# Second layer's conditioning columns as tensor-engine products inside the recurrence

## The chip, the cores and the metric

One core of a Trainium2 chip runs the whole program. The metric is device time in microseconds (us) of one execution. Engine names in this text: PE is TensorE (matmul), PEld its weight loads, DVE is VectorE, ACT is ScalarE, POOL is GpSimd, SP is SyncE, whose queue carries nearly all loads.

## What is computed

A decoder trunk of two layers on 256 tokens of width 1024, all in float32. Each layer is a mixer and a mixture of experts (MoE), each with a gated residual. The conditioning vector c (1024 numbers) enters through one product per layer:

```python
cond = jax.nn.silu(c)
for layer in range(DEPTH):
    mod = cond @ ada_w[layer] + ada_b[layer]          # (1024) @ (1024, 6144)
    sh1, sc1, g1, sh2, sc2, g2 = jnp.split(mod, 6, axis=-1)
    h = modulate(rms_norm(x, norm_mix[layer]), sh1, sc1)
    y = ...                                           # the layer's mixer
    x = x + g1[:, None, :] * y
    h = modulate(rms_norm(x, norm_ffn[layer]), sh2, sc2)
    x = x + g2[:, None, :] * grouped_moe(h, ...)
return rms_norm(x, final_norm)
```

The second layer's mixer is a linear recurrence over the tokens (RWKV-7) beside a multi-scale pooling; both are concatenated and mapped by one output projection. `grouped_moe` has 16 experts, two per token.

## The kernel before

**Conditioning.** The 6144 outputs of one layer are 12 groups of 512 (`n` = 0 to 11), and a group is four columns of the tile `modc`, with the feature on the partition. `ada(l, n)` (L194) loads a group as two tiles of 128 x 2048 (1 MB each). For each of four halves DVE multiplies 128 x 1024 weights by `cond`, which lies broadcast over the partitions, and sums along the row (L200). GpSimd then adds the bias (L204). `ada_pieces` (L206) gives the same as four pieces that the mixer hands out one at a time, each pinned behind an instruction of the recurrence. In the second layer groups 0 to 2 are done in the first layer's mixer and group 3 before its MoE. Groups 4 to 11 are done in `mixer1`: 4 and 5 are the gate of the mixer (g1), 6 and 7 sh2, 8 and 9 sc2, 10 and 11 g2.

**Order.** PE and SP run in the order in which the program is written. DVE, ACT and POOL are put in order by the tile scheduler, except where `issue_after` pins an instruction. Tiles come from rotating buffers; a load waits on SP until the buffer's last reader is done.

**`mixer1` (L1199).** Projections of the tokens (products of three split parts, L437), then decay, keys and scores, then the recurrence in four chunks `c` of 64 tokens. `each` (L1427) is the small product of the recurrence: eight products of 64 x 64, 16 records in the trace, all at L1431. The order from L1609 on is: bonus and pool products, `tok_v` and `c_r`; then two rounds (m = 16, 32) of four `level_a` and four `level_b`, in which PE and DVE answer each other; then `c_u` and `c_w` for four chunks; then `c_h`, `c_s`, `c_y`, `c_g`, `c_q` and `head_norm` chunk by chunk.

**Fill.** `Fill` (L305) is a queue of units of PE work with an estimated cost each. `run(us)` emits units until their costs reach `us`. `pace(us, every)` adds up `us` and emits one unit when the sum is over `every`. The units here are bonus and pool products (0.5 each) and units of the output projection (`OutProj.units`, 0.86 each: one product of 512 columns, L363). The projection has 16 units for the first 128 tokens (`ou`) and 16 for the others (`ou1`); the last eight of each need the finished recurrence. `heat(n)` (L177) is n products of zeros on PE.

**Then** `into_moe` (L843) takes the last eight units of `ou1` as `us`, transposes x, routes the tokens and gathers them; `moe` (L950) runs eight pairs of experts. Its weights are loaded ahead into 19 buffers and one more as these come free.

```python
            for c in range(4):
                ins = level_a(c, m, st)
                fill.pace(0.65, 0.75)
                if c % 2 and todo:
                    todo.popleft()(ins)          # one quarter of an ada group
```

Of the kernel before, what the change touches and what calls it, by code (L numbers as in the profile page):

```python
# [11 lines left out]
F32 = mybir.dt.float32  # L12
# [3 lines left out]
AF = mybir.ActivationFunctionType  # L16
OP = mybir.AluOpType
# [79 lines left out]
def trunk(ctx: ExitStack, tc: tile.TileContext, A, out):  # L97
# [58 lines left out]
    def load_consts(pool, g, eng):  # L156
        cons[g] = pool.tile([128, _CW[g]], F32, name=g)
        eng.dma_start(cons[g], A[g])

    load_consts(con, "c_all", nc.scalar)  # L160

    def K(name):
        g, o, n = _COFF[name]
# [7 lines left out]
    V.memset(epsc[:, 1:2], LNX_EPS)  # L171
    junk = con.tile([128, 1], F32, name="junk")
    junk2 = con.tile([128, 512], BF, name="junk2")
    zb = con.tile([128, 128], BF, name="zb")
    V.memset(zb, 0.0)

    def heat(n):  # L177

        if n:
            t = ps(4, 128)  # L180
            for _ in range(n):
                mm(t, zb, zb[:, None, :].to_broadcast([128, 4, 128]), start=True, stop=True)
# [8 lines left out]
    def ada_load(l, n):  # L191
        return [stream(A["ada_w"][l, n, h]) for h in range(2)]

    def ada(l, n, tiles=None, h0=0, cs=(0, 1)):  # L194

        for h, w in enumerate(tiles or ada_load(l, n), h0):
            for c in cs:
                ws = w[:, c * D:(c + 1) * D]
                k = n * 4 + h * 2 + c
                V.scalar_tensor_tensor(ws, ws, 1.0, cond, op0=OP.mult, op1=OP.mult, accum_out=modc[:, l, k:k + 1])  # L200
        if h == 0 or c == 0:
            return
        o = V_ADAB + l * 48 + n * 4
        G.tensor_tensor(modc[:, l, n * 4:n * 4 + 4], modc[:, l, n * 4:n * 4 + 4], vec[:, o:o + 4], op=OP.add)  # L204

    def ada_pieces(l, n):  # L206

        tiles = ada_load(l, n)

        def piece(h, c, after):  # L210
            with tc.issue_after(after):
                ada(l, n, [tiles[h]], h, (c,))

        return [lambda after, h=h, c=c: piece(h, c, after) for h in range(2) for c in range(2)]

    def ada_col(l, j, ct=None):
        v = modc[:, l, j * 8:j * 8 + 8]
        return v if ct is None else v[:, ct:ct + 1]

    class Rms:  # L220

# [621 lines left out]
    def into_moe(l, us, tmp):  # L843

        norm = Norm(l, 1)
        for h in range(2):
            norm.ab(h)
        route = Route(norm)
        gb2 = act.tile([128, D], F32, name="gb", tag="gb")
        gu = gate_units(l, 5, gb2)  # L850
        us = deque(u for _, u in us)
        n = len(us)

        def run(n):
            for _ in range(n):
                us.popleft()()

        if l == 0:
            for h in range(2):
                norm.rms.square(0, h)  # L860
                route.transposes(0, h)
            run(max(0, n - 12))
            for h in range(2):
                route.logits(0, h)
            route.score(0)
            norm.split_lo(0)
            route.choose(0)
            run(len(us) - 4)
            route.place(0)
            for _, u in gu:  # L870
                u()
            route.transposes(1, 0)
            norm.rms.square(1, 0)
            run(2)

            Pp = picks(route, 0, (0,))
            run(2)
            route.logits(1, 0)
            preload(AF.Sqrt, norm.rms.ss[:, 1, 0:1])
            pgs = [ps(2, 256) for _ in range(4)]  # L880
            for ct in range(4):
                gather_mm(norm, pgs, Pp, ct, 0, ct % 2 == 0)
            route.transposes(1, 1)
            for ct in range(4, 8):
                gather_mm(norm, pgs, Pp, ct, 0, ct % 2 == 0)
            norm.rms.square(1, 1)
            route.logits(1, 1)
            route.score(1)
            route.choose(1)
            heat(14)  # L890
            route.place(1)
            ada(1, 3)
        else:
            def tr(tt, h):
                norm.rms.square(tt, h)
                route.transposes(tt, h)

            tr(0, 0)
            tr(0, 1)
            run(4)  # L900
            for h in range(2):
                route.logits(0, h)
            route.score(0)
            norm.split_lo(0)
            route.choose(0)
            run(4)
            tr(1, 0)
            route.logits(1, 0)

            preload(AF.Sqrt, norm.rms.ss[:, 1, 0:1])  # L910
            pgs = [ps(2, 256) for _ in range(4)]
            tr(1, 1)
            route.logits(1, 1)
            route.score(1)
            route.place(0)
            Pp = picks(route, 0, (0,))
            route.choose(1)
            for ct in range(8):
                gather_mm(norm, pgs, Pp, ct, 0, ct % 2 == 0)
            for _, u in gu:  # L920
                u()
            heat(4)
            route.place(1)
        return norm, route, gb2, Pp, pgs

# [24 lines left out]
    def moe(l, norm, route, gb, Pp0, pgs0):  # L950
# [62 lines left out]
        def s_gu(p):  # L1013
            XT = st[p][0]
            res = []
            for nm in ("moe_g", "moe_u"):
                ws = {(h, e): None for h in range(2) for e in range(2)}
                for h in range(2):
                    for e in range(2):
                        ws[h, e] = stream_w(nm, p, h, e)  # L1020
                pg = ps(512)
                for kt in range(8):
                    for e in range(2):
                        mm(pg[64 * e:64 * e + 64, :], XT[:, kt, 64 * e:64 * e + 64], ws[kt // 4, e][:, (kt % 4) * 512:(kt % 4 + 1) * 512],  # L1024
                           start=kt == 0, stop=kt == 7)
                res.append(pg)
            sg = mp.tile([128, 512], F32, name="sg", tag="sg")
            P.activation(sg, res[0], AF.Silu)  # L1028
            V.tensor_tensor(sg, sg, res[1], op=OP.mult)  # L1029
            sgs.append(sg)  # L1030

# [167 lines left out]
    def mixer1(rms, xs, gs_, after):  # L1199
# [67 lines left out]
        kk, sq = big("kk"), big("sq")  # L1267
        for ct in range(4):
            P.activation(sq[:, ct], kR[:, ct], AF.Square, scale=vc(V_KK, ct))
        rest = deque(range(4, 12))  # L1270
        ada(1, rest.popleft())
        gs_.append(Parts(1792, 512, ((None, None), (None, None)), (V, V)).split())

        sg, av, gg = big("sg"), big("av"), big("gg")
# [260 lines left out]
        def c_h(c):  # L1535
            Sst["p"] = t = ps(4, 64)
            each(t, 1, lambda p, h, own, other: KB[:, c, h, p], lambda p, h, own, other: VU[:, c, h, p], c == 0)
# [37 lines left out]
                    gs_[4].split((c + 1) // 2)  # L1575
        solved = []
        gb = buf["vR"]
        todo = deque()
        for _ in range(3):
            todo.extend(ada_pieces(1, rest.popleft()))  # L1580
        st = {}
        spent, steps = 0, 0

# [25 lines left out]
        step(fill.all())  # L1609
        op = OutProj(lambda kt: gg[:, kt] if kt < 4 else oB[:, kt - 4], "wout1", gb).load(1)  # L1610
        ou, ou1 = op.units(0), op.units(1)
        todo[0](solved[0])
        todo.popleft()
        fill.add([(0.5, lambda ct=ct: bonus(ct)) for ct in range(4)])
        fill.add([(0.5, lambda g=g: pool_unit(g)) for g in range(4)])
        fill.add(ou[:8] + ou1[:8])
        for u in [lambda cs=cs: tok_v(cs) for cs in ((0, 1), (2, 3))] + [lambda c=c: c_r(c) for c in range(4)]:
            step(fill.run(0.9) + 1)
            u()
            if len(todo) > 8:  # L1620
                todo.popleft()(solved[0])
        step(1e6)
        fill.run(5.7)
        for m in (16, 32):
            for c in range(4):
                ins = level_a(c, m, st)
                fill.pace(0.65, 0.75)
                if c % 2 and todo:
                    todo.popleft()(ins)
                elif m == 16 and c == 0:  # L1630
                    for k in range(4):
                        out_mask(k)
            for c in range(4):
                ins = level_b(c, m, st)
                fill.pace(0.65, 0.75)
                if c % 2 and todo:
                    todo.popleft()(ins)
        while todo:
            todo.popleft()(ins)
        for c in range(4):  # L1640
            c_u(c)
            if c:
                c_w(c)
            fill.run(0.5)
        ada(1, rest.popleft())
        op.load(0)
        c_h(0)
        c_s(0)
        c_y(0)
# [7 lines left out]
        c_h(1)  # L1657
        c_s(1)
        c_y(1)
        ada(1, rest.popleft())  # L1660
        c_q(3)
        fill.run(1)
        head_norm(1)
# [1 line left out]
        c_s(2)  # L1665
        fill.add(gate_units(1, 2, gb) + ou[8:])
        c_y(2)
        ada(1, rest.popleft())
        fill.run(2.5)
        head_norm(2)  # L1670
        c_y(3)
        fill.run(1)
        head_norm(3)
        ada(1, rest.popleft())
        fill.run(1)
        fill.all()
        after(ou1[8:], buf["uu"])
# [29 lines left out]
def pack(i):  # L1707
# [15 lines left out]
    A["router_b"] = f(i["router_b"])  # L1723
    A["final_norm"] = f(i["final_norm"])
    aw = i["ada_w"].reshape(2, D, 12, 2, 2, 128)
    A["ada_w"] = f(aw.transpose(0, 2, 3, 5, 4, 1).reshape(2, 12, 2, 128, TW))

    def groups(w, sizes):
# [37 lines left out]
```

## Time and profile before

| | |
|---|---|
| runs | 815.93, 809.97, 811.97 us; median 811.97 |
| profiled execution | 816.05 us, of which the span from first to last instruction is 814.3 us |
| PE busy | 745.0 us (91% of the span) |
| DVE busy | 430.5 us (53%) |
| ACT busy | 227.6 us (28%) |
| DMA | 291.34 MB, mean 358 GB/s |
| mean granted TensorE clock | 0.975 |

The stretches of the second layer in the span: projections and scores from about 411 us, the recurrence from about 507 to 569 us, `into_moe` to 597 us, the second MoE to 796 us, the final norm to the end. Times in rows are us from the span's start. A fp32 product is two records of PE. Rows that say "issue" are time in which the engine waited for nothing that the profile shows.

### The profile page before, as it was taken

The numbers are of one execution on the slowest core, as the hardware profiler recorded it, in microseconds if no ns is written. First come the engines' busy times: TensorE is split into PE (matmuls) and PEld (weight loads), VectorE is DVE, ScalarE is ACT, GpSimd is POOL, SyncE is SP. The second block draws the span as 40 slices with busy tenths as digits, with TensorE's granted clock in tenths as the row PEclk, the third lists the DMA queues.
The fourth block names the chain that finished last, engine by engine and source line by source line (L and its number), as shares of the span: only waits on it lengthen the run. The fifth ranks groups of instructions, "written<-read, shape, count | busy, mean of one in ns | idle before, by whom it ended". The sixth has DMA issues, their size and how long they took to land. (4 is left out here: it accounts for less than half of the span.)

```text
span 814.3 us, 12038 instructions
## 1 busy us (share of the span) xinstructions
PE 745.0 (91%) x4814; PEld 416.3 (51%) x4815; DVE 430.5 (53%) x969; ACT 227.6 (28%) x459; POOL 9.1 (1%) x32
## 2 busy tenths in 40 slices
PE   0998989998999999999979988998899999999993
PEld 0556766546344353443358988565543535335331
DVE  5657669965114342143468978798621531334325
ACT  3021323434111020120267644312621202112012
POOL 0000000000000000000000000000000000000000
PEclk9999989999999999999999989999899999999997
DMA  9999977999899999999667285587979999999981
GB/s 360 423 424 427 425 278 272 346 385 427 343 427 427 424 427 425 427 427 426 287 232 297 104 310 210 207 299 306 415 310 425 428 425 426 426 428 425 427 345 54
DMA packets 42688, 291.34 MB, mean 358 GB/s; under 512 B 4864, under 2 KB 5504, under 8 KB 8448
## 3 DMA queue, kind: packets, MB, share of 16 engines
q1 hardware_dynamic: 41760, 288.07, 86.4%
q10 hardware_dynamic: 864, 2.40, 0.8%
q8 instruction: 42, 0.69, 0.3%
q14 instruction: 22, 0.18, 0.1%
HBM read 289.40 MB, written 1.05 MB: 357 GB/s over the span
## 5 line engine op out<-in xcount | busy, mean ns | idle before, releaser
L1024 PE MATMUL ps<-w,XT 128*64 128x512 f32 x1024 | 223.1, 594 | 0.0
L1024 PEld LDWEIGHTS ps<-w,XT 128*64 128x64 f32 x1024 | 73.5, 137 | 145.7 <-issue 144.7
L200 DVE SCALAR_TENSOR_TENSOR w<-w,cond 128x1024 f32<-128x1024 f32 x96 | 114.5, 1218 | 10.8 <-ACT cond L148 6.3
L1029 DVE TENSOR_TENSOR sg<-sg,ps 128x512 f32<-128x512 f32 x16 | 11.0, 687 | 198.6 <-PE ps L1024 198.6
L1056 PE MATMUL ps<-w,HT 128*64 128x512 f32 x512 | 113.8, 596 | 1.3 <-ACT HT L1043 1.3
L1056 PEld LDWEIGHTS ps<-w,HT 128*64 128x64 f32 x512 | 35.2, 137 | 70.5 <-issue 62.9
L363 PE MATMUL ps<-w,slab 128*128 128x512 f32 x128 | 60.7, 613 | 0.0
L437 PE MATMUL ps<-hT,wr 128*128 128x256 f32 x288 | 54.9, 293 | 5.2 <-DVE wr L391 3.7
L1070 DVE SCALAR_TENSOR_TENSOR Y<-ps,gw,Y 128x512 fp32r<-128x512 f32 x32 | 24.0, 751 | 61.7 <-ACT Y L1069 61.7
L1069 ACT ACTIVATE Y<-ps,gw 128x512 fp32r<-128x512 f32 x32 | 22.0, 686 | 101.0 <-PE ps L1056 101.0
L437 PEld LDWEIGHTS ps<-hT,wr 128*128 128x128 f32 x288 | 46.3, 198 | 6.7 <-ACT wr L389 3.1
L374 DVE TENSOR_TENSOR x<-x,ps 128x512 f32<-128x512 f32 x72 | 46.3, 681 | 0.3
L568 PE MATMUL ps<-hT,w 128*128 128x256 f32 x192 | 46.3, 399 | 0.0
L373 DVE TENSOR_TENSOR ps<-ps,gb 128x512 f32<-128x512 f32 x64 | 41.5, 692 | 2.5 <-PE ps L1085 2.4
L437 PE MATMUL ps<-lo,wr 128*128 128x256 f32 x144 | 41.6, 289 | 0.1
L1085 PE MATMUL ps<-Y,CT 128*128 128x512 f32 x128 | 39.1, 422 | 2.8 <-ACT Y L1069 1.7
L568 PEld LDWEIGHTS ps<-hT,w 128*128 128x128 f32 x192 | 37.5, 200 | 6.2 <-issue 0.8
L482 PE MATMUL ps<-w,hT 128*128 128x512 f32 (+1 forms) x96 | 37.0, 546 | 0.3 <-ACT hT L271 0.2
L1028 ACT ACTIVATE sg<-ps 128x512 f32<-128x512 f32 x16 | 9.6, 597 | 92.3 <-PE ps L1024 92.3
L363 PEld LDWEIGHTS ps<-w,slab 128*128 128x128 f32 x128 | 23.3, 194 | 22.9 <-issue 21.8
L271 ACT ACTIVATE XT<-ps,AB 128x256 f32<-128x256 f32 x32 | 17.5, 563 | 59.3 <-PE ps L937 50.8
L937 PEld LDWEIGHTS ps<-Pp,hl 128*128 128x128 f32 x224 | 28.1, 195 | 5.8 <-issue 4.9
(321 smaller groups left out, 851.8 us busy)
## 6 DMA issues: line engine op xcount, KB each, us to landing
w<-in_moe_g_dram SPq DMA_DIRECT2D x64, 1024.0 KB, 15.7
w<-in_moe_u_dram SPq DMA_DIRECT2D x64, 1024.0 KB, 15.9
w<-in_moe_d_dram SPq DMA_DIRECT2D x60, 1024.0 KB, 14.0
w<-in_ada_w_dram SPq DMA_DIRECT2D x48, 1024.0 KB, 7.9
w<-in_w_dram SPq DMA_DIRECT2D x19, 1024.0 KB, 11.9
w<-in_wout_dram SPq DMA_DIRECT2D x8, 1024.0 KB, 11.2
w<-in_cmp_w_dram SPq DMA_DIRECT2D x4, 1024.0 KB, 18.9
w<-in_moe_d_dram SPq DMA_DIRECT2D x4, 512.0 KB, 17.8
```

The source lines that it names most:

```text
L200: V.scalar_tensor_tensor(ws, ws, 1.0, cond, op0=OP.mult, op1=OP.mult, accum_out=modc[:, l, k:k + 1])
L363: mm(st[h], self.oT(kt)[:, tt * 128:(tt + 1) * 128], self.ws[h][kt // 4][:, (kt % 4) * 512:(kt % 4 + 1) * 512], start=kt == 4, stop=kt == 3)
L373: V.tensor_mul(po, po, gb[:, sl])
L374: V.tensor_add(x[:, tt, sl], x[:, tt, sl], po)
L437: mm(pq, a, b, start=first and kt == kts[0] and i == 0, stop=last and kt == kts[-1] and i == 2)
L482: mm(self.pq[tt], hT[:, kt, tt * 128:(tt + 1) * 128], self.w[:, k * n:(k + 1) * n], start=kt == 0, stop=kt == 7)
L568: mm(st["pq"], w(kt, ct * 128, ct * 128 + 128), hT[:, kt, :], start=kt == 0, stop=kt == 7)
L937: mm(pgs[ct // 2][:, ct % 2], norm.parts[tt][:, i, ct * 128:(ct + 1) * 128], Pp[:, tt].rearrange("p e s -> p (e s)"), start=start and i == ...
L1024: mm(pg[64 * e:64 * e + 64, :], XT[:, kt, 64 * e:64 * e + 64], ws[kt // 4, e][:, (kt % 4) * 512:(kt % 4 + 1) * 512], start=kt == 0, stop=k ...
L1056: mm(py[64 * e:64 * e + 64, :], HT[:, c, 64 * e:64 * e + 64], ws[e][:, c * 512:(c + 1) * 512], start=c == 0, stop=c == 3)
L1070: V.scalar_tensor_tensor(Y[:, 1, sl], py, gw, Y[:, 0, sl], op0=OP.mult, op1=OP.subtract)
L1085: mm(po, CT[:, tt], Y[:, i, h * 512:(h + 1) * 512], start=i == 0, stop=i == 1)
```

## The change

Groups 4 to 11 of the second layer are no longer DVE products. `ada_p` holds their weights in another order (input feature on the partition), in as many tiles of the same size. `ccol` holds c as eight columns, its Silu taken in the first MoE, and a ninth column with a one on partitions 0, 32, 64 and 96. `ada_units(n)` loads a group's two tiles and returns three fill units:

- `rows(0)` and `rows(1)`: four products each, a column of `ccol` broadcast to 32 stationary columns against 512 weight columns, into four blocks of 32 partitions of one PSUM bank. After `rows(1)` ScalarE copies the bank to SBUF.
- `columns`: four products with 128 columns of that copy stationary against the ninth column, which sum the four blocks; then DVE adds the bias.

The units of groups 4 to 9 go among the output projection's in the fill queue, group 10 is added after the `c_u` loop, group 11 is run in `into_moe`, where `heat(4)` goes. `pace` runs at every call (0.6 instead of 0.75).

```diff
+    ccol = con.tile([128, 9], F32, name="ccol")
+    nc.scalar.dma_start(ccol[:, 0:8], A["c_t"])
...
+    V.memset(ccol[:, 8:9], 0.0)
+    for q in range(4):
+        V.memset(ccol[32 * q:32 * q + 1, 8:9], 1.0)
...
+    def ada_units(n):
+        tiles = [stream(A["ada_p"][n - 4, h]) for h in range(2)]
+        st = {}
+        def rows(h):
+            if h == 0:
+                st["p"] = ps(512)
+            for q in range(4):
+                k = 4 * h + q
+                mm(st["p"][32 * q:32 * q + 32, :], ccol[:, k:k + 1].to_broadcast([128, 32]), tiles[h][:, q * 512:(q + 1) * 512],
+                   start=h == 0, stop=h == 1)
+            if h:
+                st["r"] = act.tile([128, 512], F32, name="arow", tag="Pp")
+                P.copy(st["r"], st["p"])
+        def columns():
+            pc = ps(4)
+            for c in range(4):
+                mm(pc[:, c:c + 1], st["r"][:, c * 128:(c + 1) * 128], ccol[:, 8:9], start=True, stop=True)
+            o = V_ADAB + 48 + n * 4
+            V.tensor_tensor(modc[:, 1, n * 4:n * 4 + 4], pc, vec[:, o:o + 4], op=OP.add)
+        return [(0.9, lambda: rows(0)), (0.9, lambda: rows(1)), (0.6, columns)]
...
             route.logits(1, 0)
+            for _ in range(2):
+                gaps.popleft()[1]()
...
             route.logits(1, 1)
+            gaps.popleft()[1]()
             route.score(1)
             route.place(0)
...
-            heat(4)
             route.place(1)
...
             P.activation(sg, res[0], AF.Silu)
+            if l == 0 and p == 0:
+                P.activation(ccol[:, 0:8], ccol[:, 0:8], AF.Silu)
...
-        rest = deque(range(4, 12))
-        ada(1, rest.popleft())
...
-        todo = deque()
-        for _ in range(3):
-            todo.extend(ada_pieces(1, rest.popleft()))
+        au = {n: ada_units(n) for n in (4, 5, 6, 7)}
...
-        todo[0](solved[0])
-        todo.popleft()
         fill.add([(0.5, lambda ct=ct: bonus(ct)) for ct in range(4)])
         fill.add([(0.5, lambda g=g: pool_unit(g)) for g in range(4)])
-        fill.add(ou[:8] + ou1[:8])
+        for n in (8, 9):
+            au[n] = ada_units(n)
+        fill.add(au[4] + ou[:8] + au[5] + ou1[:4] + au[6] + ou1[4:8] + au[7] + au[8] + au[9])
         for u in [lambda cs=cs: tok_v(cs) for cs in ((0, 1), (2, 3))] + [lambda c=c: c_r(c) for c in range(4)]:
             step(fill.run(0.9) + 1)
             u()
-            if len(todo) > 8:
-                todo.popleft()(solved[0])
         step(1e6)
         fill.run(5.7)
         for m in (16, 32):
             for c in range(4):
                 ins = level_a(c, m, st)
-                fill.pace(0.65, 0.75)
-                if c % 2 and todo:
-                    todo.popleft()(ins)
+                fill.pace(0.65, 0.6)
...
             for c in range(4):
                 ins = level_b(c, m, st)
-                fill.pace(0.65, 0.75)
-                if c % 2 and todo:
-                    todo.popleft()(ins)
-        while todo:
-            todo.popleft()(ins)
+                fill.pace(0.65, 0.6)
         for c in range(4):
             c_u(c)
             if c:
                 c_w(c)
             fill.run(0.5)
-        ada(1, rest.popleft())
         op.load(0)
+        fill.add(ada_units(10))
+        gaps.extend(ada_units(11))
```

Three more `ada(1, rest.popleft())`, after c_y(1), c_y(2) and head_norm(3), go as well.

## Rows read from the trace of the kernel before

**Rows 1.** The page: PE's busy tenths and the DMA rate in 40 slices.
```profile
PE   0998989998999999999979988998899999999993
GB/s 360 423 424 427 425 278 272 346 385 427 343 427 427 424 427 425 427 427 426 287 232 297 104 310 210 207 299 306 415 310 425 428 425 426 426 428 425 427 345 54
```

**Rows 2.** Stretches: length, busy PE, PEld, DVE, ACT, POOL (instructions), clock, DMA share, GB/s.
```profile
515.09:526.34 11.25, 11.25 (x56) 5.02 (x58) 6.17 (x13) 2.48 (x7) 1.32 (x2) 1.00 0.87 337
526.34:540.80 14.46, 13.83 (x267) 9.43 (x266) 13.51 (x29) 0.00 (x0) 0.20 (x1) 1.00 0.61 211
540.80:558.63 17.83, 14.50 (x357) 12.27 (x358) 15.74 (x38) 5.13 (x13) 0.52 (x2) 1.00 0.82 305
558.63:568.81 10.18, 10.18 (x61) 5.49 (x60) 9.31 (x19) 3.62 (x8) 0.29 (x2) 1.00 0.86 331
597.42:795.53 198.11, 197.44 (x991) 83.05 (x992) 61.24 (x110) 31.89 (x51) 0.00 (x0) 1.00 0.96 403
```

**Rows 3.** Chain of waits from 500 to 572 us, shares by line.
```profile
by line: PE ps L1431 28.2%; PE ps L363 18.1%; DVE w L200 15.1%; DVE pool L1483 4.2%; issue 4.1%; DVE slab L1443 3.3%; PE ps L1498 2.9%; PE ps L1340 2.8%; PE ps L1557 2.4%; DVE slab L1445 2.0%; DVE Wm L1437 1.9%; DVE pool L1492 1.8%; DVE ps 
```

**Rows 4.** The longest of PE's three waits from 597 us: total, times, longest.
```profile
PE ps L1085 <- ACT Y L1069: 0.9, 1, 0.9
```

**Rows 5.** L200's instructions (ns min/median/max), then pieces of the chain (start, us, what).
```profile
L200 DVE SCALAR_TENSOR_TENSOR w<-w,cond x96: 1177/1220/1235, 8.7 to 567.4; 128x1024 f32<-128x1024 f32 x96
...
531.69 1.14 DVE w L200 x2
...
556.90 1.29 issue
...
563.31 2.37 DVE w L200 x4
...
568.64 1.21 DVE ps L373 x2
...
571.76 0.38 PE ps L771
```

**Rows 6.** Table of stretches, as in rows 2, for group 4's place.
```profile
440.00:470.00 30.00, 30.00 (x283) 27.29 (x286) 26.88 (x45) 22.08 (x38) 0.20 (x1) 1.00 0.34 122
```

**Rows 7.** Chain of waits in into_moe.
```profile
573.87 4.37 PE ps L363 x8
578.24 1.69 PE ps L790 x16
579.93 3.53 PE ps L363 x8
...
588.70 3.27 PE ps L937 x16
...
593.26 0.86 PE ps L182 x4
```

**Rows 8.** Chain of waits where PE has no gap: lone and grouped units.
```profile
517.00 0.61 PE ps L1431 x16
...
520.14 6.21 PE ps L363 x14
526.34 1.08 PE ps L1431 x32
527.42 1.06 PE ps L363 x2
```

**Rows 9.** Timeline of PE in the first layer's compression: start, us, line, tile, shapes.
```profile
67.78 1.93 PE L607 MATMUL ps<-w,slab 128*32 128x256 f32 x32 [1.90 <-DVE slab L550]
69.64 1.09 PE L592 MATMUL ps<-c_all,slab 128*128 128x128 f32 x8
```

**Rows 10.** Groups by line and shape: a ScalarE copy (busy us, mean ns | idle before).
```profile
L340 ACT COPY slab<-ps 128x512 f32<-128x512 f32 x4 | 2.2, 589 | 2.6 <-PE ps L339 2.6
```

**Rows 11.** Table of stretches, as in rows 2, behind the mixer's end.
```profile
572.00:574.00 2.00, 2.00 (x11) 2.00 (x11) 0.69 (x4) 1.99 (x3) 0.00 (x0) 0.55 1.01 416
```

**Rows 12.** Timeline of SP's loads: the first of the second MoE.
```profile
537.05 1.07 SPq L134 DMA_DIRECT2D w<-in_moe_g_dram  x2
```

More of the change, by code (lines that the diff above doesn't have):

```diff
@@ L204, in ada @@
         G.tensor_tensor(modc[:, l, n * 4:n * 4 + 4], modc[:, l, n * 4:n * 4 + 4], vec[:, o:o + 4], op=OP.add)
[L206 to L214, printed above, removed]
+    def ada_units(n):
[18 more added lines that the diff above has]
+        return [(0.9, lambda: rows(0)), (0.9, lambda: rows(1)), (0.6, columns)]
     def ada_col(l, j, ct=None):
@@ L218, in ada_col @@
         return v if ct is None else v[:, ct:ct + 1]
+    gaps = deque()
     class Rms:
@@ L1626, in mixer1 @@
                 ins = level_a(c, m, st)
-                fill.pace(0.65, 0.75)
-                if c % 2 and todo:
-                    todo.popleft()(ins)
-                elif m == 16 and c == 0:
+                fill.pace(0.65, 0.6)
+                if m == 16 and c == 0:
                     for k in range(4):
@@ L1659, in mixer1 @@
         c_y(1)
-        ada(1, rest.popleft())
         c_q(3)
@@ L1667, in mixer1 @@
         c_y(2)
-        ada(1, rest.popleft())
         fill.run(2.5)
@@ L1673, in mixer1 @@
         head_norm(3)
-        ada(1, rest.popleft())
         fill.run(1)
@@ L1725, in pack @@
     aw = i["ada_w"].reshape(2, D, 12, 2, 2, 128)
+    A["ada_p"] = f(i["ada_w"][1].reshape(2, 4, 128, 12, 512)[:, :, :, 4:].transpose(3, 0, 2, 1, 4).reshape(8, 2, 128, TW))
+    A["c_t"] = f(i["c"].reshape(8, 128).T)
     A["ada_w"] = f(aw.transpose(0, 2, 3, 5, 4, 1).reshape(2, 12, 2, 128, TW))
```

## Prediction

> **What bounds the kernel now.** I read the page's totals and slices first: TensorE (PE) is busy in nine tenths of nearly every slice [rows 1], VectorE (DVE) in 53% of the span. A busy share is an average, so I went to the stage that the change touches, the second layer's recurrence, by the table of stretches [rows 2]. From 515.09 to 526.34 us PE has no idle time at all; from 526.34 to 540.80 it is idle for 0.63 of 14.46 us, from 540.80 to 558.63 for 3.33 of 17.83, and from 558.63 to 568.81 not at all. DVE is nearly full there too (13.51, 15.74, 9.31). Two engines are loaded side by side, and the reader should ask which one can give way. The chain of waits from 500 to 572 us answers in part [rows 3]: DVE's conditioning products (L200) hold 15.1% of these 72 us, 10.9 us, against 46% for PE's L1431 and L363. So about 11 us is all that taking L200 out can return. The rest of the chain is PE work that stays.
>
> Behind it, into_moe runs from 571.76 to 597.42, and the second MoE then runs on PE alone: idle 0.67 of 198.11 us [rows 2]. PE has three waits there, none of them for a transfer [rows 4]. So the end moves one for one with the moment at which the mixer hands over.
>
> **What is removed.** 32 DVE products with their accumulator reads (8 column groups of 4). The trace has 96 of these at a median of 1.22 us [rows 5]; one takes about 1.14 us net of overlap (1.14 for product and read in the chain [rows 5]), so 32 x 1.14 = 36.5 us of DVE work goes. Eight small GpSimd additions go too. The four products of group 4 lie at 441 to 447 us, where PE runs through without a gap (30.00 of 30.00 us [rows 6]): nothing gained. The other 28 lie after 508 us. heat(4), 0.86 us of PE [rows 7], goes.
>
> **What is added on PE, unit by unit.** A group is two rows units (four products each, 32 stationary and 512 moving columns, in four column blocks) and one columns unit (four products with 128 stationary columns and one moving one). Seven groups run in the mixer (14 rows, 7 columns), one in into_moe.
>
> A rows unit: if its four products run side by side it is as long as one product of 512 columns, 6.21 / 7 = 0.89 us where seven follow one another [rows 8]; if not, four times that. The nearest row is the compression stage's L607, also four blocks of 32 columns: 16 products of 256 columns take 67.78 to 69.64, 1.86 us [rows 9]. Four products of 512 columns are half of that, 0.93 us. I take 0.93; the ends are 0.85 and 1.06 (one lone unit [rows 8]).
>
> The Trainium skill speaks less well of packing: "TensorE: Matmul & The Clock Gate", section "Measured speedup vs the span model", gives 3.07 times for four packed tiles, not four. An estimate by that page would be 4 x 0.89 / 3.07 = 1.16 us a unit and 16 x 0.23 = 3.7 us more in all. L607 is the same packing in this kernel and shows no such loss, so this stays out of the sum.
>
> A columns unit: the nearest row is L790, 16 records (eight products with 128 stationary columns) in 1.69 us [rows 7], so 0.85 us for four; the ends are half of it, 0.42, and a lone unit's 1.06.
>
> Dense sum in the mixer: 14 x 0.93 + 7 x 0.85 = 19.0 us.
>
> **Insertion.** A unit alone between two small-product groups costs more than one in a run. Sixteen L1431 records take 0.61 us alone and 1.08 for two groups; a lone L363 unit takes 1.06 against 0.89 [rows 8]. So a lone unit costs 0.17 to 0.19, and the split pair 0.07: 0.26. The pace line now runs a unit at each of the 16 level steps, where before one ran at every second step until the queue was empty, five in all. With four more in the c_u loop, some 15 more units stand alone: 15 x 0.26 = 3.9 us; the four groups of units placed later add 4 x 0.26 = 1.0.
>
> **The new wait.** columns needs ScalarE's copy of the row sums; a copy of that shape takes 0.59 us [rows 10]. In the level loop 0.6 us of other products cover it. Twice (group 8 after c_y(0), group 10 after c_y(2)) columns follows rows at once: 2 x 0.65 = 1.3 us. PE's queue runs in order, so the next c_g, c_q and head_norm stand behind it. Where ScalarE is busy it is longer.
>
> Added on PE: 19.0 + 4.9 + 1.3 = 25.2 us.
>
> **What PE had to spare.** With L200 gone, DVE answers at once. From 526.34 to 540.80 the bare work is 16 step groups at 0.54 and five lone units at 1.06, 13.9 us; 0.5 is spare. From 540.80 to 568.81 I count 24 small groups (13.0), four norm products (0.43 each, 1.7), two gate units (1.0) and eight output units at 0.85 (6.8): 22.5 of 28.0 us, so 5.5 spare. Together 6.0 us, of which PE shows 3.96 as idle [rows 2]; these are the two ends. I take 6.0, since the new units stand in just those waits. PE then ends the mixer's part 25.2 - 6.0 = 19.2 us later.
>
> **The tail.** Before, PE's last output product ended at 568.81, but DVE was on group 11 from 563.31 to 568.64, then added the result to x and made the router's factors until 571.76 [rows 5]. What would be late next without L200 is the last pair of L373 and L374, about 1.3 us; L771 and the first transposes go ahead of it. Gain 2.2 us. After these 2.95 us without PE work the granted clock was 0.55 (1.2 GHz for most of the two us) [rows 11], and four output units took 4.37 us where the next four took 3.53 [rows 7]: 0.8 us. A gap of 1.3 us (556.90 to 558.19 [rows 5], in a stretch with clock 1.00 [rows 2]) shows no such fall, so I count 0.8 as gained. Sum 3.0.
>
> **into_moe.** Two rows units, one columns unit and two insertions, less heat: 1.86 + 0.85 + 0.52 - 0.86 = 2.4 us. They stand between logits and place(0), on the way to the first gather (L937 at 588.70 [rows 7]).
>
> **Costed at nothing.** The conditioning tiles are as many and as large; they are now freed by PE. The MoE weights queue on SP behind the loads of groups 10 and 11, which now wait for rows and output units: they begin at about 553 to 560 instead of 537.05 [rows 12], but the first MoE product is later too (about 615 instead of 597.42). At 427 GB/s [rows 1] a tile of 1.05 MB takes 2.5 us, so the twenty early ones need 49 us and have 55. Were that cover gone, PE would wait for the last of them, some 5 us. The 9-column load, five memsets and one 8-column Silu lie beside other work at the start and in the first MoE; the eight row copies lie on ScalarE, which is busy for at most 5.13 us of a stretch [rows 2].
>
> **Sum:** 19.2 - 3.0 + 2.4 = +18.6 us. The profiled execution took 816.05 us (1.75 of it outside its span of 814.3), so it would take 834.7; its time lies 4 above the median of the runs, 811.97. Set on the median, 831 us.
>
> **Rivals.**
> *DVE set the pace (faster).* If the recurrence is held by DVE's queue and the new products fit into PE's waits, the 10.9 us of L200 in the chain and heat's 0.86 come back: 800 us. For it: L200 stands in the chain at 531 to 543 and 563 to 568 us [rows 5]. Against it: it needs 25 us of room on PE, where I count 6 and see 4 idle. It decides if a rows unit costs under some 0.2 us.
> *Hidden room (no change that can be measured).* PE's busy time may hide room: 16 x 0.85 + 8 x 0.42 = 17.0 us of work, nothing for insertion, less 2.3 us of overhead in 515 to 541 (25.7 us for 16 x 0.85 and 18 x 0.54), 5.5, 3.0 and 0.86 gives +5: 817 us. For it: weight loads fill only 9.43 of 14.46 us [rows 2]. Against it: what an insertion costs is seen [rows 8].
> The Trainium skill says in "Perfetto Trace Analysis", section "Identifying the Most-Contended Engine", that matmul busy time is no good measure of how full TensorE is; by that rule this rival stands better than the idle times alone let it, and the 2.3 us of overhead inside gapless stretches agree with it that far.
> *The blocks do not run side by side.* Then a rows unit costs 3.5 us: 16 x 2.5 = 40 more, 870 us. L607 speaks against it [rows 9].
>
> **How the numbers follow.** Chances: forecast 0.80, DVE 0.05, hidden room 0.10, no packing 0.05. About 1% (8.1 us) is what a measurement can tell from no change. The forecast's ends: low, rows 0.85, columns 0.42, lone units 0.19, no copy wait, 6.0 spare, 3.0 tail: 14.8 + 2.9 - 9.0 + 1.3 = +10.0, 822. High, 1.06 for every unit, 4.0 spare, no clock gain, a table load's 1.3 us of wait in into_moe: 22.3 + 6.2 - 4.0 - 2.2 + 4.1 = +26.4, 838. The runs spread by some 3 us about their median; with that and the hidden-room case the range is 817 to 842. Faster 0.05, same 0.12 (hidden room and the forecast's lowest end), slower 0.83.
>
> **What would show it.** Right: PE busy without a gap through the recurrence, L200 gone after 420 us, eight records of a rows unit in 0.9 to 1.1 us, the levels ending some 10 us later, the last output product 19 us later, the first MoE product about 615, the MoE as long as before. Wrong: rows units much shorter or longer, PE idle still there in the levels, or PE waiting for a MoE weight.

## The result and the profile after

Four executions of each kernel side by side gave 840.67 us (837.19 to 841.99) after, against 813.91 us (809.97 to 815.93) before: ratio 1.0336, 95% interval 1.0302 to 1.0370. The forecast was 831 us in a range of 817 to 842, with slower as the likeliest side. After is 26.8 us longer than before, which is past the forecast's own high end of +26.4; the time is inside the range because the range allowed for the spread of the runs. So the question is where some 8 us more than the sum of +18.6 came from, and whether the terms of the sum held one by one.

The profiled execution took 841.43 us, 839.7 of them its span; before it was 816.05 and 814.3. The page after: busy time of the engines and PE's slices (before: [rows 1]).

```profile
PE 768.0 (91%) x5002; PEld 425.2 (51%) x5003; DVE 398.6 (47%) x918; ACT 235.4 (28%) x470; POOL 5.8 (1%) x24
PE   0799889998999999999889899999999999999993
```

A line number of after stands 23 to 27 above that of before, for the lines named here: L1456 is L1431, L386 is L363, L962 is L937, L1049 is L1024. In the experiments it is a few lines more or less again. L222 and L231 are the new rows and columns products, L226 the copy between them. This is the table of stretches after, from the recurrence on: length, busy PE, PEld, DVE, ACT, POOL (instructions), clock, DMA share, GB/s (before: [rows 2]).

```profile
525.26:530.52 5.26, 5.26 (x15) 2.11 (x16) 0.16 (x1) 0.00 (x0) 0.00 (x0) 1.00 0.62 257
530.52:557.25 26.73, 26.43 (x327) 14.26 (x328) 8.95 (x23) 1.17 (x2) 0.00 (x0) 1.00 0.53 197
557.25:587.34 30.09, 28.62 (x497) 19.71 (x498) 10.67 (x31) 10.18 (x23) 0.00 (x0) 1.00 0.90 323
594.22:596.51 2.29, 1.28 (x11) 1.08 (x11) 1.48 (x3) 1.27 (x3) 0.00 (x0) 1.00 0.98 415
596.51:622.29 25.78, 23.04 (x128) 16.93 (x129) 14.82 (x60) 14.23 (x26) 0.00 (x0) 0.87 0.85 337
622.29:821.00 198.71, 198.03 (x992) 82.89 (x992) 61.21 (x110) 32.48 (x52) 0.00 (x0) 1.00 0.97 402
```

DVE, busy 13.51 of 14.46 us in the levels before, is busy for 8.95 of 26.73 there now, and PE is idle for 0.30 us there. The MoE is as long as before. The chain of waits (start, us, what) from the recurrence on shows the pieces:

```profile
520.90 1.00 PE ps L222 x8
521.90 0.61 PE ps L1456 x16
523.57 0.59 ACT arow L226
524.21 1.05 PE ps L231 x8
525.26 5.26 PE ps L386 x12
...
587.34 6.88 PE ps L386 x16
594.25 0.70 DVE ps L396
...
596.51 3.44 PE ps L386 x8
...
613.29 3.79 PE ps L962 x16
...
622.29 13.02 PE ps L1049 x59
```

The extra 25.4 us of the span are read by landmarks that both traces have. The recurrence begins with this group, before and then after:

```profile
507.26 1.28 PE ps L1431 x20
```
```profile
513.08 1.18 PE ps L1456 x20
```

So 5.82 us are lost before the part that the change is about. From there to the second MoE's first product it is 109.21 us in place of 90.16: 19.05 us. From that product to the end, 0.53.

Most of the 5.82 us arises in the first 30 us of the kernel. ScalarE's timeline (start, us, line, operation, shapes, and in brackets the idle time before it and what ended it), after:

```profile
8.58 0.47 ACTq L162 DMA_DIRECT2D ccol<-in_c_t_dram  x1
...
12.30 1.28 ACT L1055 ACT_TABLE_LOAD   x1
21.84 0.21 ACT L1055 ACTIVATE ccol<-ccol 128x8 f32<-128x8 f32 x1 [8.26 <-DMA ccol<-in_c_t_dram]
21.96 0.61 ACT L250 ACTIVATE junk<-x 128x512 bf16<-128x512 f32 x1
...
24.19 1.28 ACT L255 ACT_TABLE_LOAD   x1
```

Before, the third square (L227 there) is the last whose data came late:

```profile
15.28 0.63 ACT L227 ACTIVATE junk<-x 128x512 bf16<-128x512 f32 x1 [2.33 <-DMA x<-in_x_dram]
```

The eight-column Silu (L1055) is written in the first MoE, whose own Silus begin at 211 us (in e1, below). It depends only on a 4 KB load, so the scheduler that orders each engine's instructions put it near the head of ScalarE's queue, ahead of three of the four squares (L250) of the first norm. That load took 13.2 us to land. It stands right behind that of c_all in the same queue (186 KB, 13.1 us); whether it waited for that one or for the megabytes of weights on SP's queue, no run here shows. ScalarE loaded another table, stood still for 8.26 us, and loaded a table again behind the squares. PE's first projection product (L505) starts at 28.65 us, before (L482) at 23.19: 5.46 us. The Trainium skill says in "Perfetto Trace Analysis", section "Tensor Engine Instruction (MATMUL, LD_WEIGHTS)", that ScalarE's queue is strictly first in, first out; this trace agrees, since that data had landed by 15.3 us in before's trace, and the squares behind the Silu still began at 21.96.

A second piece of ScalarE's order moved at 446 us: the cast of the fourth gate slab (L412) runs at 446.34, ahead of copies that PE waits for, and the distance from L460's group of 96 products to its next group grew from 18.34 to 19.53 us, 1.19 more. The first of these groups starts at 432.98 us, before at 428.36, so 0.84 of the 5.46 us had been made good by then: 4.62 and 1.19 are the 5.82, but for rounding.

### The profile page after: what moved, and what is told of

Its sections match the earlier page's. It is cut to its first block, busy times and chain, and to the rows that moved or that the text cites. A ratio compares the mean times of both kernels' runs of the same rounds, so it can differ in the third digit from the quotient of the medians.

```text
span 839.7 us, 12373 instructions
## 1 busy us (share of the span) xinstructions
PE 768.0 (91%) x5002; PEld 425.2 (51%) x5003; DVE 398.6 (47%) x918; ACT 235.4 (28%) x470; POOL 5.8 (1%) x24
## 3 DMA queue, kind: packets, MB, share of 16 engines
HBM read 289.40 MB, written 1.05 MB: 346 GB/s over the span
## 5 line engine op out<-in xcount | busy, mean ns | idle before, releaser
L1049 PE MATMUL ps<-w,XT 128*64 128x512 f32 x1024 | 223.7, 595 | 0.0
L1049 PEld LDWEIGHTS ps<-w,XT 128*64 128x64 f32 x1024 | 73.5, 138 | 146.5 <-issue 144.9
L205 DVE SCALAR_TENSOR_TENSOR w<-w,cond 128x1024 f32<-128x1024 f32 x64 | 76.0, 1217 | 7.5 <-ACT cond L148 5.9
L386 PE MATMUL ps<-w,slab 128*128 128x512 f32 x128 | 60.1, 606 | 0.0
L460 PE MATMUL ps<-hT,wr 128*128 128x256 f32 x288 | 55.1, 293 | 4.9 <-DVE wr L414 3.7
L460 PEld LDWEIGHTS ps<-hT,wr 128*128 128x128 f32 x288 | 46.5, 198 | 6.7 <-ACT wr L412 3.1
L460 PE MATMUL ps<-lo,wr 128*128 128x256 f32 x144 | 41.8, 290 | 0.0
L505 PE MATMUL ps<-w,hT 128*128 128x512 f32 (+1 forms) x96 | 37.2, 548 | 0.1
L386 PEld LDWEIGHTS ps<-w,slab 128*128 128x128 f32 x128 | 22.7, 190 | 22.0 <-issue 21.0
L962 PEld LDWEIGHTS ps<-Pp,hl 128*128 128x128 f32 x224 | 28.6, 199 | 5.7 <-issue 4.9
```

What stands on the lines that cost most here:

```text
L386: mm(st[h], self.oT(kt)[:, tt * 128:(tt + 1) * 128], self.ws[h][kt // 4][:, (kt % 4) * 512:(kt % 4 + 1) * 512], start=kt == 4, stop=kt == 3)
L460: mm(pq, a, b, start=first and kt == kts[0] and i == 0, stop=last and kt == kts[-1] and i == 2)
L505: mm(self.pq[tt], hT[:, kt, tt * 128:(tt + 1) * 128], self.w[:, k * n:(k + 1) * n], start=kt == 0, stop=kt == 7)
L962: mm(pgs[ct // 2][:, ct % 2], norm.parts[tt][:, i, ct * 128:(ct + 1) * 128], Pp[:, tt].rearrange("p e s -> p (e s)"), start=start and i == ...
```

## The experiments

The medians of before were 812.03 us in the session of e1 to e4, 813.06 in that of e5 to e8, and 813.49 in the last. Ratios are against the runs of the same session.

**e1: the Silu held back.** After, with the new Silu put behind the first MoE's own.

```diff
-            P.activation(sg, res[0], AF.Silu)
+            d = P.activation(sg, res[0], AF.Silu)
             if l == 0 and p == 0:
-                P.activation(ccol[:, 0:8], ccol[:, 0:8], AF.Silu)
+                with tc.issue_after(d.ins):
+                    P.activation(ccol[:, 0:8], ccol[:, 0:8], AF.Silu)
```

> The changed kernel with one edit: the Silu of the 8-column tile is pinned behind the Silu of the first expert pair in the first MoE, so that the scheduler cannot put it at the head of ScalarE's program. Theory (start stall): of the 25.4 us by which the changed kernel's profiled execution is longer, 5.5 us arise because that Silu stands third on ScalarE and waits 8.3 us for its load; the first projection product then starts at about 23.2 us instead of 28.65, the first MoE product of the second layer at about 617 instead of 622.3, and the time is 5 to 6 us shorter than the changed kernel's, ratio to the kernel before about 1.026. Rival (absorbed): the first layer waits for its weights anyway, the early delay is made good before the second layer and something else shifts it; then the ratio stays at 1.033.

Measured: 833.79 us, ratio 1.0257 [1.0212, 1.0302]. The squares follow one another from 11.50 us, PE's first projection product starts at 23.03, the recurrence at 507.25 and the second MoE at 616.46. The same 109.21 us lie between those two as in after. So the start is worth about 6 us (5.8 between the profiled executions), and nothing else hangs on it.

**e2: the Silu alone.** Before, with only the load of the c columns and their Silu added, read by nobody.

```diff
+    ccol = con.tile([128, 9], F32, name="ccol")
+    nc.scalar.dma_start(ccol[:, 0:8], A["c_t"])
...
+            if l == 0 and p == 0:
+                P.activation(ccol[:, 0:8], ccol[:, 0:8], AF.Silu)
```

> The kernel before with the 8-column load and its unpinned Silu added, and nothing else of the change (nothing reads the result). Theory (start stall): 5 to 6 us slower than before, ratio 1.006 to 1.008, with the first projection product near 28.6 us. Rival (absorbed): ratio 1.000 to 1.002.

Measured: 821.54 us, ratio 1.0106 [1.0073, 1.0140]. ScalarE's timeline at its start:

```profile
12.37 1.28 ACT L1032 ACT_TABLE_LOAD   x1
21.95 0.21 ACT L1032 ACTIVATE ccol<-ccol 128x8 f32<-128x8 f32 x1 [8.29 <-DMA ccol<-in_c_t_dram]
22.06 0.61 ACT L229 ACTIVATE junk<-x 128x512 bf16<-128x512 f32 x1
```

Two instructions that compute nothing anyone uses cost 1%. The stall is the same as in after, to 0.1 us. The time is some 3 us more than the 5 to 6 expected, and that goes with the clock granted to the single executions: e2's at a mean clock of 0.981 took 816.11 us, where before's five at 0.981 took 810.51 to 811.26; e2's at 0.971 took 821.54, where before's five at 0.971 took 815.60 to 816.55. In these pairs e2 is 4.9 to 5.9 us longer.

The profiled execution is that of 816.11 us, and its second layer is the code of before, so it serves as another trace of it, with less time lost to the clock:

```profile
510.33 1.33 PE ps L1435 x20
...
574.35 3.44 PE ps L365 x8
...
596.97 13.88 PE ps L1026 x64
```

From the recurrence to the MoE's first product it takes 86.64 us, where before's own trace takes 90.16.

**e3: DVE relieved, PE not loaded.** Before, with the second layer's products of groups 4 to 11 cut to 2 of 1024 columns (their sums are left out but for these two).

```diff
-                ws = w[:, c * D:(c + 1) * D]
+                m = 2 if l and n > 3 else D
+                ws = w[:, c * D:c * D + m]
```

> The kernel before with the DVE products of groups 4 to 11 cut from 1024 to 2 columns each; the loads, the waits and the order stay, and these columns' sums are left out, so the modulation of the second MoE is another. It measures what freeing DVE is worth without any new PE work. Theory (PE holds the recurrence): at most the room that the prediction counted, 6.0 us in the recurrence, 2.2 in the tail and 0.8 of clock, so 6 to 9 us faster, 805 to 807 us against 813. Rival (DVE set the pace): 11 us or more faster, 802 us or less.

Measured: 809.59 us, ratio 0.9965 [0.9943, 0.9986]: 2.8 us. That is about the most that the change could have brought by taking the products off DVE, and under a third of the 9.0 that the prediction credited; the 6 to 9 us expected of e3 did not come. The chain of waits shows why:

```profile
506.84 0.80 PE ps L1432 x20
...
535.51 1.06 PE ps L364 x2
536.57 5.83 PE ps L1432 x190
542.40 0.98 issue
543.38 3.83 PE ps L1432 x113
...
548.34 0.96 issue
549.30 2.20 PE ps L1432 x55
...
565.75 0.70 DVE ps L374
...
590.67 13.88 PE ps L1025 x64
```

PE's small products now follow one another through the whole recurrence; what gaps remain (0.98, 0.96) wait for nothing that the profile shows. From 506.84 to the last output product's end, 565.73, it is 58.89 us, with PE busy for 56.59. DVE's 32 products were in the chain of before, but behind them PE's own chain was nearly as long. From the recurrence to the MoE it is 83.83 us, 2.81 under e2's trace, as much as the runs give: 0.6 of it up to DVE's first update behind the recurrence, 2.2 from there to the MoE.

**e4: half as long rows.** After, with each row product on 256 of 512 columns (the other half of the sums is left out; the row copy becomes two of half the width).

```diff
-                mm(st["p"][32 * q:32 * q + 32, :], ccol[:, k:k + 1].to_broadcast([128, 32]), tiles[h][:, q * 512:(q + 1) * 512],
+                mm(st["p"][32 * q:32 * q + 32, 0:256], ccol[:, k:k + 1].to_broadcast([128, 32]), tiles[h][:, q * 512:q * 512 + 256],
```

> The changed kernel with each rows product on 256 of its 512 moving columns (half of the sums are left out; the row copy becomes two copies of half the width). Theory (each us of PE work in the recurrence is a us of time): a rows unit falls from 1.00 to about 0.58 us, 16 x 0.42 = 6.8 us less, of which nearly all shows: ratio about 1.025. Rival (hidden room, the units fill waits): 0 to 3 us less, ratio 1.030 to 1.033.

Measured: 833.13 us, ratio 1.0266 [1.0226, 1.0306], 5.7 us under after by the ratios. A rows unit takes 0.57 us in place of 1.00, and 16 x 0.43 = 6.9. So most of what is taken off a unit comes off the end: PE's time there is time on the path. In the trace, from the recurrence's start to the end of the last output product, it is 74.20 us in place of 81.14, 6.94 less, where the 14 units there give 6.0 and the copies that PE waits for are shorter too.

**e5: the cast later.** e1, with the split of the fourth gate slab behind the copies.

```diff
-        gs_.append(Parts(1792, 512, ((None, None), (None, None)), (V, V)).split())
+        gs_.append(Parts(1792, 512, ((None, None), (None, None)), (V, V)))
...
+        with tc.issue_after(dg.ins), tc.issue_after(dr.ins):
+            gs_[3].split()
```

> The changed kernel with the Silu of the c columns pinned behind the first MoE's Silu (as in e1_silu_pinned), and the split of the fourth gate slab (gs_[3]) moved behind the last copy of gg and the last maximum of rn. Theory: of the extra time left in e1 about 1.2 us comes from that slab's cast, which with the DVE products of group 4 gone goes ahead of the copies at 445 to 451 us. The distance from L460's first group of 96 products to the next of 183 goes back from 19.5 to about 18.3 us, and the time is about 1.2 us under e1's 833.8: 832 to 833 us, ratio about 1.0245. Rival: ScalarE has slack there that is used up later anyway, or the cast is then late for its own products: same as e1 or up to 1.5 us over it, ratio 1.025 to 1.028.

Measured: 834.75 us, ratio 1.0280 [1.0234, 1.0326], no gain over e1. The wait itself went: from L460's group (427.73 us) to its next (446.08) it is 18.35 us, in e1 19.52 (427.16 to 446.68), and e1's wait of 0.6 us for DVE at L1316 is gone. But a new one came; PE's waits from 430 to 520 us (total, times, longest):

```profile
PE ps L460 <- DVE wr L414: 2.9, 1, 2.9
PE ps L1459 <- DVE slab L1283: 1.9, 1, 1.9
PE ps L1430 <- ACT slab L1409: 0.9, 1, 0.9
```

The third line is not in e1. It cost less than was won: from L460's group to the recurrence it is 79.23 us (427.73 to 506.96), in e1 80.09, in before 78.90. So 0.9 of the 1.2 us came back in the trace, and the medians of executions that spread by 4 us do not show it.

**e6: no packing.** e1, with all eight row products of a group into one and the same block of 32 partitions; the copy and the column products then go by that block alone.

```diff
-                mm(st["p"][32 * q:32 * q + 32, :], ...
-                   start=h == 0, stop=h == 1)
+                mm(st["p"][0:32, :], ...
+                   start=h + q == 0, stop=h == 1 and q == 3)
```

> As e1_silu_pinned, but with all eight row products of a unit chain in one and the same block of 32 output partitions, one after the other, and no second step over four blocks. Theory: the four products of a unit run side by side only because they write to different row blocks. Then a unit of four goes from 1.00 us to about 4 x 0.86 = 3.4 us, the 16 units add about 16 x 2.4 = 38 us to TensorE in the recurrence, and since nothing there has that much to hide behind, the time is about 833.8 + 35 = 869 us (860 to 875), ratio about 1.07. Rival: the four are four-byte products held by something other than the array (their moving columns' read), so that the packing brings little: unit 1.0 to 1.3 us, time 834 to 839 us.

Measured: 875.08 us, ratio 1.0773 [1.0712, 1.0835]. In its chain of waits:

```profile
512.65 3.55 PE ps L222 x8
516.20 0.61 PE ps L1457 x16
516.81 3.56 PE ps L222 x8
```

3.55 us for the same four products that take 1.00 side by side: 16 x 2.55 = 40.8 us, and the time rose by 41.3 (two executions). The packing is real, worth 3.55 times, and every microsecond of a unit shows up at the end.

**e7: two units at a time.** e1, with two fill units at every second level step.

```diff
+                self.run(0.01)
...
-                fill.pace(0.65, 0.6)
+                fill.pace(0.65, 1.2)
```

> As e1_silu_pinned, with the fill work of the levels let out in two units at every second level step in place of one at each. Theory: a unit that stands alone among the level products pays an insertion of about 0.26 us that two together share (0.61 + 1.06 us for a step with a unit against 1.85 us for two units together and 1.11 less for the step). About 8 fewer insertions give back 2 us on TensorE: time 831 to 832.5 us, ratio about 1.023. Rival: the time is the units' own, and a step without a unit waits for DVE's copies (the level's own chain shows through), so that what is saved comes back as waits: 833 to 837 us, ratio 1.025 to 1.030.

Measured: 833.91 us, ratio 1.0258 [1.0212, 1.0304]: no difference from e1 that these four executions can tell. Its trace does show the saved insertions, in the levels:

```profile
526.32 1.08 PE ps L1458 x32
527.39 1.91 PE ps L387 x4
529.31 1.08 PE ps L1458 x32
530.38 1.85 PE ps L222 x16
```

The eight pairs run to 551.26, 24.94 us; e1's sixteen single steps run from 524.69 to 552.03, 27.34. From recurrence to MoE it is 2.9 us shorter than e1 (106.34), of which 1.1 is a faster granted clock at the gather (2.68 us for L963, 3.78 in e1). The time lies in the rival's range, but the waits for DVE that the rival asks for are not in the trace. The profiled spans differ by 1.3 us, the medians by nothing; whether 2 us are there I can't settle with runs that spread by 4.

**e8 and e9: the work moved, not its engine.** If DVE's products cost 2.8 us where they are, moving a few of them might beat before. In e8, a version of before, the products of groups 10 and 11, from which the second MoE's gate is made, wait for the MoE's first modulate, and the gate's products go behind the first pair's down products. In e9 group 10's go into DVE's gaps ahead of the router and only group 11's wait. Both also move one early load of the MoE's weights forward in the order and give the final norm's weights a tile of their own; what that does alone was not run.

```diff
-        ada(1, rest.popleft())
+        held.append((10, ada_load(1, 10)))
...
+                    with tc.issue_after(norm.mod.ins):
+                        for n, t in held:
+                            ada(1, n, t)
...
+            if l and p == 0:
+                for _, u in gate_units(l, 5, gb):
+                    u()
```

> The kernel before with one thing altered: the VectorE products of groups 10 and 11, of which the second MoE's gate is made, are held back from the recurrence's end into the MoE's first pair, behind its modulate, and the gate's products go behind the first pair's down products. Theory: what DVE has to do in the recurrence's end costs little there (taking all products of groups 4 to 11 away brought 2.8 us), so a quarter of them brings 0.7 us, and the gate's 1.29 us of products moved off the stretch ahead of the MoE another 1 us: 809.5 to 811.5 us, ratio 0.996 to 0.999. Rival: eight products of 1.1 us on DVE in the MoE come between the products of gate and up projections and their evictions, and TensorE waits: 812 to 818 us, ratio 1.000 to 1.007.

> As e8_late_gate, but group 10's VectorE products run in DVE's gaps ahead of the router (behind the second update of x), and only group 11's four wait for the MoE's first modulate, so that two weight buffers are held until about 595 us and not four until 600. Theory: e8 lost its gain because the MoE's weight loads stood still for about 16 us (a stretch of 8 and 0 GB/s) while four buffers were held, and the loads, at 425 GB/s through the whole MoE, can't make that up; TensorE then waited 7.1 us for weights. With half the buffers held half as long the loads stand still some 8 us, which the kernel before's slack covers, no wait for weights shows in the MoE, and the gain at the MoE's start (first product at about 590 us in e8, 597 in the profile of before) comes through: 808.5 to 811 us, ratio 0.995 to 0.998. Rival: any hold of a buffer costs as much as the gate brings: 813 to 817 us, ratio 1.000 to 1.005, with waits for weights of 2 to 4 us.

Measured: e8 820.83 us, ratio 1.0101 [1.0063, 1.0140]; e9 815.13 us, ratio 1.0025 [1.0000, 1.0051]. e8 lies above both of its ranges, e9 in its rival's. In e8 the MoE's first product starts at 589.68 us, before at 597.42, as hoped, and the gain is lost behind it: from there to the end it takes 12.4 us longer than before. The held products' weight buffers belong to the ring that the MoE's weights go through. Tables of stretches of e8 and of before, then e8's first waits of PE from 560 us:

```profile
563.00:571.00 8.00, 6.99 (x25) 3.57 (x24) 3.90 (x9) 4.81 (x8) 0.00 (x0) 1.00 0.00 0
```
```profile
563.00:571.00 8.00, 5.81 (x15) 2.47 (x13) 8.00 (x17) 1.42 (x3) 0.20 (x1) 1.00 0.97 399
```
```profile
PE ps L1026 <- DMA w<-in_moe_u_dram: 5.2, 4, 2.5
PE ps L1026 <- DMA w<-in_moe_g_dram: 1.9, 2, 1.2
```

The loads stand still where before moved 399 GB/s, and later PE waits 7.1 us for weights, where before waits for none. SP's longest wait there, 20.5 us, ends in e8 with PE's output products (L365), and in e9, 19.2 us, with group 10's own products on DVE. e9 holds half as many buffers; the same 8 us stand still, the wait falls to 3.4 us, and its first MoE product is at 592.70. Neither beats before: a buffer held is a transfer late.

**e10: before once more,** for a second trace of it.

> The kernel before as it is, for a second profile of it. Theory: its recorded profile is one from the slow end (its 816 us against a median of 812 to 813), and its recurrence has 3 us that e2_before_silu's lacks: a gap of 1.29 us that nothing explains, and a slower clock behind a wait of 3.0 us of TensorE. A second profile has a span of 809 to 812 us and the MoE's first product 594 to 597 us. Rival: those 3 us are the kernel's own: span 813 to 815 us and the first product at 597 to 598 us.

Measured: 816.26 us, span 814.5, the MoE's first product at 597.63: the rival. The gap of 1.29 us [rows 5] is not in this trace, and the recurrence up to DVE's first update is 59.11 us (507.34 to 566.45; 61.38 in the first trace). But the way from there to the MoE takes 31.18 us in place of 28.78:

```profile
572.08 5.24 PE ps L363 x8
577.31 1.69 PE ps L790 x16
579.00 3.53 PE ps L363 x8
```
```profile
572.00:574.00 2.00, 2.00 (x4) 0.88 (x3) 0.69 (x1) 1.99 (x3) 0.00 (x0) 0.50 1.03 377
```

The clock granted there is 0.50 (1.2 GHz), after 3.0 us in which PE waited for DVE. In e2, the same recurrence with the same wait (2.9 us), the four units took 3.44 us and the whole way 27.09. So after one and the same wait the clock fell in two executions and not in a third.

## Why the prediction came out as it did

**The side was right, and for the reason given; the size was not.** The time rose by 26.8 us, 8.2 more than the sum and just past its high end. PE was the engine without room: e6 raised the time by what its units grew, e4 lowered it by most of what they shrank. The rivals fall: DVE did not set the pace (e3: 2.8 us for all of L200, where that rival wanted 10.9); PE did not hide the units (+5 us); the blocks run side by side (1.00 us a unit, against 3.55).

**The step that failed** is in "Costed at nothing": "one 8-column Silu lie[s] beside other work at the start and in the first MoE". It was costed where the text of the kernel has it, not where ScalarE would run it. It cost about 6 us (after less e1) and is most of the difference between +18.6 and the measured +26.8. The rest lies mostly in "What PE had to spare", below.

**The cast at 446 us** was under "nothing gained" for group 4's products, because PE has no gap there [rows 6]. In after the order of the casts changed and 1.2 us were lost in the trace; in e5, with the cast put back, 0.9 of them returned. Why the order changed is not shown: in e3, where the same products are cut short but still there, the distance stays 18.34 us.

**The sum from recurrence to MoE** came out in part by luck: +18.6 forecast, +19.05 between the profiled executions, +18.92 against e10's trace, but +22.6 against e2's (109.21 less 86.64). Before's two profiled executions (816.05 and 816.26 us) are from the slow end of its runs, and by the runs' times of e3 and e1 it is +21.4, all told. So the sum was 3 to 4 us short. Its parts:
- *Rows and columns units:* 0.93 and 0.85 forecast; alone between small products 1.00 and 1.05, two rows units together 1.85 us. With the small products' 0.61 a level step takes 1.61 to 1.67, a little under the forecast (0.54 + 0.93 + 0.26 = 1.73).
- *Added on PE:* 25.2 us forecast. After against e3, where DVE is out of the way in both, the recurrence is 81.17 less 58.89 = 22.3 us longer. PE is busy there for 79.28 us against 56.59, 22.7 more, where units and insertions were forecast at 23.9. Its waits for the row copies, 1.5 us, were forecast at 1.3 and added nothing: PE is idle for 1.86 us there, in e3 for 2.30.
- *What PE had to spare:* 6.0 us forecast. e3 against the two traces of before gives 2.7 and 0.2 us to the last output product or DVE's first update (58.89 and 58.91 against 61.55 and 59.11); e2's trace gives 0.6 (59.55). So this is the term that was mis-sized most. I counted 36.4 us of bare work from 526.34 to 568.81, small groups at their best pitch of 0.54. e3 needs 39.83 for the same stretch (525.90 to 565.73). The pieces of its chain there add up to 37.3 us of products, 0.9 more than I counted, and 2.5 of gaps that DVE has no part in: 2.1 of them wait for nothing that the profile shows, 0.4 for ScalarE. I had counted every gap of before as DVE's.
- *Tail and clock:* -3.0 forecast. After has 2.29 us from the last output product to the next where before had 5.06, a gain of 2.77, and four units in 3.44 us in place of 4.37, 0.93. Both hold in these two traces. But e10 and e2 show that what the clock takes there changes from one execution to the next: against e2, where the four units took 3.44 us already, the 0.93 is nothing. The 2.2 forecast for the tail without the clock is what e3 gives against e2.
- *into_moe:* +2.4 forecast, +3.1 (24.94 us in e3 from the last output product, 28.05 in e1). Some 0.9 of that is the clock: the gather (L962) took 3.78 us in e1 at a granted clock of 0.50, 2.86 in e3 (L938) at 0.69. The last columns unit (605.39 us in e1) stands behind the row copy, and the copy behind a table load of 1.28 us, the wait that the forecast had put into its high end.

Set on the runs' times, with the two experiments that take the parts apart: before to e3 -2.8 by the ratio (DVE relieved), e3 to e1 +24.2 by the medians (the units on PE, heat off, the cast), e1 to after +6.4 by the ratios (the Silu at the start). The forecast had -9.0, +27.6 and 0. Two errors of size, 6 on what DVE gives back and 3 on what PE is asked for, lay on opposite sides and cancelled in part, 3 us being left; the Silu had nothing against it.

## What to carry to other kernels

An instruction of an in-order engine costs what it holds up where the scheduler puts it, not where the text has it: for each small operation that is added, ask for its last dependency, and if that is early, which queue it may jump and which transfer it would wait for there. What an engine gives back by losing work is found by cutting that work short in the old kernel, not by adding up its share of a chain of waits: here 10.9 us of chain share were worth 2.8. And a stretch without idle time on TensorE takes every added product at its full length, packed or not.

## What the runs showed of the hardware

- A load of 4 KB took 13.2 us to land at the kernel's start, as long as the one of 186 KB ahead of it in the same queue (13.1). Its small size bought nothing there.
- Executions of one kernel differ with the clock that they were granted: before's five at a mean of 0.971 took 815.60 to 816.55 us, its five at 0.983 took 807.67 to 808.56. A difference of 2 us between two kernels is read at like clocks, or not at all.
- Four products with 32 stationary columns each, into four blocks of 32 partitions, took 1.00 us side by side against 3.55 one after the other in one block, 3.55 times. The Trainium skill gives 3.07 times for four packed row tiles ("TensorE: Matmul & The Clock Gate", section "Measured speedup vs the span model"); for column blocks at 512 columns this case's runs lie above it.
- After PE's wait of about 3 us for DVE the granted clock from 572 to 574 us was 0.55 in one execution and 0.50 in another, and four output units took 4.37 and 5.24 us; in e2 after the same wait they took 3.44. What decides it no run here shows.
- In the second MoE the loads run at some 425 GB/s without a stop, and the 8 us and more in which they stood still ahead of it were not made up in e8: 7.1 us of waits for weights followed, from 730 to 790 us.
